# Norms of queries and keys in one chain over four steps, softmax over three, and later loads from DRAM, in a decoder trunk on one core

## The chip, the cores and the metric

The kernel runs on one core of one Trainium2 chip. The metric is the device time of one execution in microseconds, as the median of several runs; less is better. A core has a matrix engine (TensorE, PE in the profile, with PEld for its weight loads), a vector engine (VectorE, DVE), an engine for functions of one operand (ScalarE, ACT), a general one (GpSimd, POOL) and SyncE (SP), which here only issues DMAs. Each engine works through its own instructions in the order of the program, and waits on semaphores for the others. SBUF is the working memory with 128 partitions; PSUM takes the results of matmuls; DRAM holds the weights.

## The reference

One sequence of 256 tokens, 2048 features, two layers. Layer 0 is a gated mixer of tokens in chunks, layer 1 is attention with 16 heads of 128 and forget gates; a convolutional feed-forward of width 5632 follows each. The change touches the attention alone:

```python
def fox_shared_kv(h, kv_norm, w_kvf, b_f, k_norm):
    kvf = rmsnorm(h, kv_norm) @ w_kvf
    k, v, f = ...
    k = rmsnorm(k, k_norm)              # over the 128 features of each head
    c = jnp.cumsum(log_sigmoid(f + b_f), axis=1)

def forgetting_attention(xn, w_qg, q_norm, w_out, k, v, c):
    q, g = jnp.split(xn @ w_qg, 2, axis=-1)
    q = rmsnorm(q, q_norm)              # over the 128 features of each head
    s = einsum(q, k) * scale + c[t] - c[s]      # only s <= t
    p = jax.nn.softmax(s, axis=-1)
    o = einsum(p, v) * jax.nn.sigmoid(g)
    return o @ w_out
```

Queries are taken in two blocks of 128 tokens (tb = 0 and 1): the first block sees 128 keys, the second 256.

## The kernel before

**Chunks and steps.** All weights come as a stream of chunks of 128 x 1024 numbers (512 KB). `Stream.run` (L86) walks the list of items, and each item is a step. In step i it issues the load of item i + 6 on SyncE's queue (L70), splits item i + 3 into a high part `whi` on ScalarE (L82) and the rest `wlo` on VectorE (L83), issues the matmuls of item i (L166), and then lets every pending generator run to its next `yield`, in the order in which they were started (L57). A generator that is started in a chunk's matmuls runs its first piece in the same step; one that another generator starts begins a step later. An item without weights (`then`) is a place in the list where something is started, with no advance of generators. There are four buffers for loaded chunks and four each for `whi` and `wlo`. So the order of work on each engine is fixed by the order of steps, and a `yield` more in a generator moves what follows it behind the split of one further chunk.

**The attention's items.** b_q (queries, 4 blocks of 8 chunks), the chunk of forget gates, kvf_k (keys, 4 blocks of 8), a `then` that starts `heads`, kvf_v (values, 4 blocks of 8), b_g (gates), b_out. Counted from the first chunk of b_q as step 0: queries take steps 0 to 31, forget gates 32, keys 33 to 64, values 66 to 97, gates 98 to 129. A block of queries, keys or values is 256 tokens x 512 features (4 heads), with its sums in a PSUM tile `ps` of two halves (tb); there are three such tiles.

**Queries and keys** (`head_norm`, L575). When a block's last matmul is done, for each half: Square on ScalarE (L581), a sum for each of the 4 heads (L584), mean and epsilon (L585), the inverse root by one instruction on the bits (L269) and three Newton steps of three instructions (L274 to L276), the factor of the token's own norm (L587), the product into a buffer of the group `big` (L589). A step later the transpose in 32 x 32 blocks (L551) and an `exchange` (L555): four writes to DRAM (L559), one step later the read back with the blocks in transposed places (L562), one step later what is to follow, for queries the scaled copy by `q_scaled` (L604) another step later.

**Key and value operand** (`kv_operand`, L566): sixteen `prep` (L258, L259), one a step, make the normalized residual that the forget, key and value matmuls use.

**Forget gates** (`forget_sums`, L633): some 20 steps of small pieces on VectorE after step 32.

**Heads** (`heads`, L675). A head takes two steps. In the first: the difference of the forget sums into `L` (L693, L694; from a row `cB` that GpSimd's queue fetches, L683), the mask (L696), the attention output of an earlier head (L705 to L707) and its copy (L714), the scores of this head (L711, L712) into a PSUM tile of the group `mp`, of which there are two. In the second: scale and add (L718), and for the two blocks of queries the maximum (L722) and Exp with its sum (L723), then reciprocal (L725), scaling (L727), transpose and exchange, after whose read back the head is `waiting` for its output. A head's output is made when its values are there and when its number is below n - 2, n being the head whose scores are due.

**Values** (`v_evict`, L610): two copies on ScalarE (L614) after each block. **Gates** (`g_done`, L733) wait until `state["done"]` says that the two heads which they multiply are there.

Of the kernel before, what the change touches and what calls it, by code (L numbers as in the profile page):

```python
# [10 lines left out]
F32 = mybir.dt.float32  # L11
F32R = mybir.dt.float32r
I32 = mybir.dt.int32
AF = mybir.ActivationFunctionType
OP = mybir.AluOpType
AX = mybir.AxisListType

P = 128
D = 2048
T = 256  # L20
# [3 lines left out]
NH = 16  # L24
CHUNK = 1024
EPS = 1e-6
SCALE = 128 ** -0.5
# [12 lines left out]
class Stream:  # L40
# [10 lines left out]
    def then(self, at_load=None, at_split=None, at_mult=None):  # L51
        self.items.append((None, at_mult, at_load, at_split))
# [80 lines left out]
def build(ctx, tc, d, out):  # L133
    nc = tc.nc
# [3 lines left out]
    small = ctx.enter_context(tc.tile_pool(name="small", bufs=1))  # L138
# [8 lines left out]
    rcol = const.tile([P, 2], F32, name="rcol")  # L147
# [4 lines left out]
    s = Stream(nc, wpool)  # L152
    ph = Phase(tc)
# [112 lines left out]
    def rsqrt(y, v, n):  # L266

        t = small.tile([P, n], F32, name="rs_t", tag=f"rs_t{n}", bufs=2)
        nc.vector.tensor_scalar(y.bitcast(I32), v.bitcast(I32), -0.5, 1597463007.0, op0=OP.mult, op1=OP.add)  # L269
        for _ in range(3):  # L270
            newton(y, v, t)

    def newton(y, v, t):
        nc.vector.scalar_tensor_tensor(t, y, -0.5, y, op0=OP.mult, op1=OP.mult)  # L274
        nc.vector.tensor_tensor(t, t, v, op=OP.mult)  # L275
        nc.vector.scalar_tensor_tensor(y, t, 1.5, y, op0=OP.add, op1=OP.mult)  # L276
# [270 lines left out]
    def blocks_turned(src, n):  # L547


        turned = ph.temp("turned", [P, 512])[:, :n * P].rearrange("p (c h j) -> p c h j", c=4, h=n)  # L550
        nc.vector.transpose(turned.rearrange("p c h j -> p h c j"),  # L551
                            src.rearrange("p (h c i) -> p h c i", h=n, c=4))
        return turned.rearrange("p c h j -> p c (h j)")

    def exchange(key, turned, n, new, then):  # L555

        way = dram.tile([4, 32, 4, n * 32], F32, name=f"way_{key}", tag=f"way_{key}")
        for r in range(4):
            nc.sync.dma_start(way[:, :, r, :].rearrange("c i x -> i c x"), turned[32 * r:32 * r + 32])  # L559
        yield  # L560
        dst = new()
        nc.sync.dma_start(dst, way.rearrange("c i r x -> (c i) r x"))  # L562
        yield
        then(dst)

    def kv_operand():  # L566
        att("X2")
        nc.vector.tensor_tensor(att("gain"), column(C_QNORM), column(C_KNORM), op=OP.mult)
        for _ in range(3):
            yield  # L570
        for kt in range(KD):
            prep(att("X2"), kt, C_KVNORM)
            yield

    def head_norm(key, blk):  # L575

        def done(ps):
            for tb in range(2):
                x = ps[:, tb, :]
                sq = small.tile([P, 2, T], F32, name="sq", tag="sq", bufs=2).rearrange("p a b -> p (a b)")  # L580
                nc.scalar.activation(sq, x, AF.Square, scale=rcol[:, tb:tb + 1])  # L581
                v = ph.temp("hv", [P, 4])
                r = ph.temp("hr", [P, 4])
                nc.vector.tensor_reduce(v, sq.rearrange("p (a b) -> p a b", a=4), axis=AX.X, op=OP.add)  # L584
                nc.vector.tensor_scalar(v, v, 1.0 / P, EPS, op0=OP.mult, op1=OP.add)  # L585
                rsqrt(r, v, 4)
                nc.vector.tensor_scalar(r, r, rcol[:, tb:tb + 1], None, op0=OP.mult)  # L587
                n = ph.temp("big", [P, 512], bufs=6)
                nc.vector.tensor_tensor(n.rearrange("p (a b) -> p a b", a=4), x.rearrange("p (a b) -> p a b", a=4),  # L589
                                        r[:, :, None].to_broadcast([P, 4, P]), op=OP.mult)  # L590
                yield
                turned = blocks_turned(n, 4)
                if key == "k":
                    new = lambda tb=tb: att("k").rearrange("p b t h j -> p b t (h j)")[:, blk, 4 * tb:4 * tb + 4]
                    s.start(exchange(f"k{blk}{tb}", turned, 4, new, lambda dst: None))
                else:
                    s.start(exchange(f"q{blk}{tb}", turned, 4, lambda: four_rows(4),
                                     lambda dst, tb=tb: s.start(q_scaled(blk, tb, dst))))
        return done

    def four_rows(n):
        return ph.temp("rows", [P, 512], bufs=6)[:, :n * P].rearrange("p (r x) -> p r x", r=4)

    def q_scaled(blk, tb, rows):  # L604

        yield
        nc.scalar.activation(att("q")[:, 4 * blk:4 * blk + 4, tb * P:(tb + 1) * P].rearrange(
            "p h (r j) -> p r h j", r=4), rows.rearrange("p r (h j) -> p r h j", h=4), AF.Copy, scale=att("gain"))
# [66 lines left out]
    def heads():  # L675

        q, k, v, ccol = att("q"), att("k"), att("v"), att("ccol")
        parts = [(0, 0, 1), (1, 1, 3)]
        rows, waiting = {}, []

        def fetch(hd):
            rows[hd] = ph.temp("cB", [P, T])
            nc.gpsimd.dma_start(rows[hd], cd[hd:hd + 1, :].to_broadcast([P, T]))  # L683

        fetch(0)
        yield
        n = 0
        while state["done"] < NH:
            if n < NH:
                cB = rows.pop(n)  # L690
                L = ph.temp("big", [P, 512], bufs=6)[:, :3 * P]
                l = L.rearrange("p (a b) -> p a b", a=3)
                nc.scalar.activation(l[:, 0, :], cB[:, :P], AF.Identity, scale=-1.0, bias=ccol[:, 0, n:n + 1])  # L693
                nc.scalar.activation(l[:, 1:, :], cB.rearrange("p (a b) -> p a b", a=2), AF.Identity, scale=-1.0,  # L694
                                     bias=ccol[:, 1, n:n + 1])
                nc.gpsimd.affine_select(l[:, 0::2, :], l[:, 0::2, :], pattern=[[0, 2], [-1, P]],  # L696
                                        compare_op=OP.is_ge, fill=NEG, base=0, channel_multiplier=1)
                if n + 1 < NH:
                    fetch(n + 1)
            go = [hd for hd, _ in waiting if hd < min(state["v"], n - 2)][:2 if n >= NH else 1]  # L700
            o = misc_ps() if go else None
            for i, hd in enumerate(go):
                pT = waiting.pop(0)[1]
                oo, vv = o[:, i * T:(i + 1) * T], v[:, :, hd * P:(hd + 1) * P]
                nc.tensor.matmul(oo[:, :P], vv[:, 0, :], pT[:, :, 0, :], start=True, stop=True)  # L705
                nc.tensor.matmul(oo[:, P:], vv[:, 0, :], pT[:, :, 1, :], start=True, stop=False)
                nc.tensor.matmul(oo[:, P:], vv[:, 1, :], pT[:, :, 2, :], start=False, stop=True)  # L707
            if n < NH:
                S = misc_ps()[:, :3 * P]
                kk = k[:, n // 4, :, n % 4, :]  # L710
                nc.tensor.matmul(S[:, :P], q[:, n, :P], kk[:, :4], start=True, stop=True)  # L711
                nc.tensor.matmul(S[:, P:], q[:, n, P:], kk, start=True, stop=True)  # L712
            for i, hd in enumerate(go):
                nc.scalar.activation(q[:, hd, :], o[:, i * T:(i + 1) * T], AF.Copy)  # L714
                state["done"] += 1
            yield
            if n < NH:
                nc.vector.scalar_tensor_tensor(L, S, SCALE, L, op0=OP.mult, op1=OP.add)  # L718
                mx = ph.temp("mx", [P, 2])
                sm = ph.temp("sm", [P, 2])  # L720
                for tb, a, b in parts:
                    nc.vector.tensor_reduce(mx[:, tb:tb + 1], l[:, a:b, :], axis=AX.XY, op=OP.max, negate=True)  # L722
                    nc.scalar.activation(l[:, a:b, :], l[:, a:b, :], AF.Exp, bias=mx[:, tb:tb + 1],  # L723
                                         accum_out=sm[:, tb:tb + 1])
                nc.vector.reciprocal(sm, sm)  # L725
                for tb, a, b in parts:
                    nc.vector.tensor_scalar(l[:, a:b, :], l[:, a:b, :], sm[:, tb:tb + 1], None, op0=OP.mult)  # L727
                s.start(exchange(f"p{n}", blocks_turned(L, 3), 3, lambda: four_rows(3),
                                 lambda dst, n=n: waiting.append((n, dst.rearrange("p r (b j) -> p r b j", b=3)))))
            yield  # L730
            n += 1

# [17 lines left out]
    state = {"normed": False, "layer": 0, "v": 0, "done": 0, "gates": 0}  # L750
# [100 lines left out]
```

## Time and profile before

| what | us |
|---|---|
| median of 3 runs | 2222.88 (2222.6 to 2224.47) |
| profiled execution | 2217.78 |
| its span, first to last instruction | 2216.1 |
| granted clock of TensorE, mean | 0.998 |
| DVE busy | 1481.1 |
| ACT busy | 1142.3 |
| POOL busy | 24.0 |

A row of a timeline gives start and length in us, engine, line, operation, what is written and read, shapes, count, and in brackets the idle time before it with what ended it. A row of a table of windows gives the stretch and its length, then busy time and count of instructions for PE, PEld, DVE, ACT and POOL, then the granted clock of TensorE (1.00 is full), the share of the DMA engines' time and GB/s. Ends of matmuls are modelled and overlap the next one's start. A row of the waits gives the total, how often and the longest.

### The profile page before, as it was taken

Reading aid. Unit: us, or ns where it says so; the run is one execution under the profiler, and the core shown is the slowest. Engines: PE = TensorE matmul, PEld = TensorE weight load, DVE = VectorE, ACT = ScalarE, POOL = GpSimd, SP = SyncE. Lnnn points to the kernel's source line nnn. Section 1 sums busy time; section 2 is a strip of 40 time slices with the busy share of each in tenths; the row PEclk is TensorE's granted clock in tenths of the full one; section 3 lists DMA queues with packets and bytes.
Section 4 is the critical chain, followed back from the end, with each engine's and each line's share of the span. In section 5 each row is a group of like instructions: output and inputs, shape, how many; then the busy total and the mean of one; then the engine's idle time right before and its main releaser. Section 6 shows DMA issues by size and latency. Waiting matters only on the chain.

```text
span 2216.1 us, 41701 instructions
## 1 busy us (share of the span) xinstructions
PE 2193.7 (99%) x17096; PEld 2097.0 (95%) x17096; DVE 1481.1 (67%) x2140; ACT 1142.3 (52%) x1525; POOL 24.0 (1%) x41
## 2 busy tenths in 40 slices
PE   9999999999999999999999999999999999999998
PEld 8899999999999999998777888999999999999998
DVE  6667677777777655547786766667777777764553
ACT  6545455555555544435443665545555555544443
POOL 0000000000000000000000210000000000000000
PEclk9999999999999999999999999999999999999999
DMA  8555555555555555555666776555555565555653
GB/s 306 179 189 181 198 191 195 196 191 194 196 191 192 198 192 191 189 200 185 202 205 217 240 237 194 193 186 199 192 199 191 191 199 191 194 196 192 196 191 136
DMA packets 139951, 437.39 MB, mean 197 GB/s; under 512 B 24032, under 2 KB 34672, under 8 KB 139504
## 3 DMA queue, kind: packets, MB, share of 16 engines
q1 hardware_dynamic: 138816, 432.62, 58.9%
q0 software_dynamic: 768, 2.10, 0.4%
q8 instruction: 133, 2.18, 0.4%
q14 instruction: 58, 0.48, 0.1%
q10 hardware_dynamic: 176, 0.02, 0.0%
HBM read 425.22 MB, written 9.45 MB: 196 GB/s over the span
## 4 chain that ended last, share of the span: by engine, by line
PE 90%; DVE 4%; DMA 3%; issue 1%; ACT 1%; SPq 0%; ACTq 0%; DVEq 0%; POOL 0%; POOLq 0%
PE ps L166 88%; DVE wlo L83 1%; DMA raw<-kvf_k 1%; PE mp L166 1%; DMA raw<-b_q 1%; ACT whi L82 1%; DMA way_k<-att_turned 0%; DVE att_turned L551 0%; DVE att_hv L584 0%; PE mp L489 0%; DMA raw<-kvf_v 0%; DVE rs_t L275 0%; DVE rs_t L274 0%; DVE att_hr L276 0%; DMA way_q<-att_turned 0%
## 5 line engine op out<-in xcount | busy, mean ns | idle before, releaser
L83 DVE TENSOR_TENSOR wlo<-raw,whi 128x1024 fp32r<-128x1024 f32 (+1 forms) x787 | 954.1, 1218 | 455.4 <-ACT whi L82 453.6
L82 ACT ACTIVATE whi<-raw 128x1024 fp32r<-128x1024 f32 (+1 forms) x787 | 826.2, 1056 | 693.4 <-PE ps L166 590.0
L166 PE MATMUL ps<-X,whi 128*128 128x256 f32 (+1 forms) x6176 | 826.3, 285 | 0.0
L166 PEld LDWEIGHTS ps<-X,whi 128*128 128x128 f32 x6176 | 757.9, 188 | 16.2
L166 PE MATMUL ps<-X,wlo 128*128 128x256 f32 x3328 | 445.3, 276 | 0.0
L166 PEld LDWEIGHTS ps<-X,wlo 128*128 128x128 f32 x3328 | 413.0, 188 | 5.5
L166 PE MATMUL ps<-ffn_H,whi 128*128 128x256 f32 (+1 forms) x2696 | 342.9, 277 | 0.0
L166 PEld LDWEIGHTS ps<-ffn_H,whi 128*128 128x128 f32 x2696 | 322.6, 188 | 1.1
L166 PE MATMUL ps<-ffn_H,wlo 128*128 128x256 f32 x1364 | 186.7, 276 | 0.0
L166 PEld LDWEIGHTS ps<-ffn_H,wlo 128*128 128x128 f32 x1364 | 170.2, 188 | 0.4
L166 PE MATMUL ps<-whi,att_X 128*128 128x512 f32 x512 | 167.3, 403 | 0.0
L523 DVE SCALAR_TENSOR_TENSOR ffn_c<-ffn_a,col,ffn_c 128x255 f32<-128x255 f32 x352 | 162.0, 481 | 6.3
L166 PE MATMUL ps<-whi,X 128*128 128x512 f32 x512 | 160.9, 395 | 0.0
L519 ACT ACTIVATE ffn_c<-ffn_a,col 128x256 f32<-128x256 f32 x176 | 96.5, 596 | 49.7 <-DVE ffn_a L316 49.7
L166 PEld LDWEIGHTS ps<-whi,att_X 128*128 128x128 f32 x512 | 97.6, 191 | 21.1
L166 PEld LDWEIGHTS ps<-whi,X 128*128 128x128 f32 x512 | 96.6, 189 | 20.9 <-ACT whi L82 0.3
L316 DVE TENSOR_TENSOR ffn_a<-ps,rB 128x512 f32<-128x512 f32 x74 | 51.2, 692 | 96.6 <-PE ps L166 96.6
L166 PE MATMUL ps<-wlo,att_X 128*128 128x512 f32 x256 | 101.9, 398 | 6.6 <-DVE wlo L83 6.4
L166 PE MATMUL ps<-wlo,X 128*128 128x512 f32 x256 | 99.6, 392 | 5.6 <-DVE wlo L83 5.6
L258 ACT ACTIVATE X<-h,col 128x256 fp32r<-128x256 f32 x64 | 29.2, 502 | 84.6 <-DVE h L322 67.8
L166 PE MATMUL ps<-att_X,whi 128*128 128x256 f32 (+2 forms) x520 | 68.9, 281 | 0.0
L166 PEld LDWEIGHTS ps<-wlo,att_X 128*128 128x128 f32 x256 | 49.0, 191 | 19.6 <-DVE wlo L83 9.0
(156 smaller groups left out, 1152.8 us busy)
## 6 DMA issues: line engine op xcount, KB each, us to landing
raw<-up SPq DMA_DIRECT2D x352, 512.0 KB, 3.3
raw<-down SPq DMA_DIRECT2D x176, 512.0 KB, 4.3
raw<-a_in_u SPq DMA_DIRECT2D x32, 512.0 KB, 3.6
raw<-a_out SPq DMA_DIRECT2D x32, 512.0 KB, 4.1
raw<-b_q SPq DMA_DIRECT2D x32, 512.0 KB, 4.1
raw<-kvf_k SPq DMA_DIRECT2D x32, 512.0 KB, 4.7
raw<-kvf_v SPq DMA_DIRECT2D x32, 512.0 KB, 4.8
raw<-b_g SPq DMA_DIRECT2D x32, 512.0 KB, 4.2
```

Source lines behind the costliest of these rows:

```text
L82: self.nc.scalar.activation(hi[:, :n], raw, AF.Copy)
L83: self.nc.vector.tensor_tensor(lo[:, :n], raw, hi[:, :n].bitcast(F32), op=OP.subtract)
L166: nc.tensor.matmul(o, a, b, start=start, stop=stop, skip_group_check=True)
L258: nc.scalar.activation(dst[:, kt, :T], h[:, kt, :], AF.Copy, scale=g)
L316: nc.vector.tensor_tensor(a, src, rB[:, None, :].to_broadcast([P, 2, T]), op=OP.mult)
L519: nc.scalar.activation(c[:, m, :], a[:, m, :], AF.Identity, scale=w[2], bias=column(C_CONVB + l * 2 * KF + f))
L523: nc.vector.scalar_tensor_tensor(c[:, m, n:], a[:, m, :T - n], w[k], c[:, m, n:], op0=OP.mult, op1=OP.add)
```

## The change

`exchange` has one `yield` more between its writes and its read back. `kv_operand` makes sixteen preps in 24 steps. `head_norm` takes Square and sums of both halves in its first step; in the second one chain for both (8 columns); in the third and fourth a half's product, transpose and start of its exchange each. `q_scaled` waits one step more. In `heads` the softmax is a generator of its own: scale, sum and maxima a step after the scores, both Exps a step later, reciprocal, scaling and transpose a step later, and the exchange a step after that. `heads` starts its first head two steps later, and the condition that a head's output comes at least three heads after its scores is gone; it comes as soon as the read back has been issued.

```diff
@@ -558,6 +558,7 @@
         for r in range(4):
             nc.sync.dma_start(way[:, :, r, :].rearrange("c i x -> i c x"), turned[32 * r:32 * r + 32])
         yield
+        yield
         dst = new()
         nc.sync.dma_start(dst, way.rearrange("c i r x -> (c i) r x"))
         yield
@@ -570,25 +571,29 @@
             yield
         for kt in range(KD):
             prep(att("X2"), kt, C_KVNORM)
-            yield
+            for _ in range(1 + kt % 2):
+                yield
 
     def head_norm(key, blk):
 
         def done(ps):
+            v = ph.temp("hv", [P, 2, 4])
+            r = ph.temp("hr", [P, 2, 4])
+            sq = [small.tile([P, 2, T], F32, name="sq", tag="sq", bufs=2).rearrange("p a b -> p (a b)")
+                  for _ in range(2)]
             for tb in range(2):
-                x = ps[:, tb, :]
-                sq = small.tile([P, 2, T], F32, name="sq", tag="sq", bufs=2).rearrange("p a b -> p (a b)")
-                nc.scalar.activation(sq, x, AF.Square, scale=rcol[:, tb:tb + 1])
-                v = ph.temp("hv", [P, 4])
-                r = ph.temp("hr", [P, 4])
-                nc.vector.tensor_reduce(v, sq.rearrange("p (a b) -> p a b", a=4), axis=AX.X, op=OP.add)
-                nc.vector.tensor_scalar(v, v, 1.0 / P, EPS, op0=OP.mult, op1=OP.add)
-                rsqrt(r, v, 4)
-                nc.vector.tensor_scalar(r, r, rcol[:, tb:tb + 1], None, op0=OP.mult)
+                nc.scalar.activation(sq[tb], ps[:, tb, :], AF.Square, scale=rcol[:, tb:tb + 1])
+                nc.vector.tensor_reduce(v[:, tb, :], sq[tb].rearrange("p (a b) -> p a b", a=4), axis=AX.X, op=OP.add)
+            yield
+            nc.vector.tensor_scalar(v, v, 1.0 / P, EPS, op0=OP.mult, op1=OP.add)
+            rsqrt(r.rearrange("p a b -> p (a b)"), v.rearrange("p a b -> p (a b)"), 8)
+            nc.vector.tensor_tensor(r, r, rcol[:, :, None].to_broadcast([P, 2, 4]), op=OP.mult)
+            for tb in range(2):
+                yield
                 n = ph.temp("big", [P, 512], bufs=6)
-                nc.vector.tensor_tensor(n.rearrange("p (a b) -> p a b", a=4), x.rearrange("p (a b) -> p a b", a=4),
-                                        r[:, :, None].to_broadcast([P, 4, P]), op=OP.mult)
-                yield
+                nc.vector.tensor_tensor(n.rearrange("p (a b) -> p a b", a=4),
+                                        ps[:, tb, :].rearrange("p (a b) -> p a b", a=4),
+                                        r[:, tb, :, None].to_broadcast([P, 4, P]), op=OP.mult)
                 turned = blocks_turned(n, 4)
                 if key == "k":
                     new = lambda tb=tb: att("k").rearrange("p b t h j -> p b t (h j)")[:, blk, 4 * tb:4 * tb + 4]
@@ -596,6 +601,7 @@
                 else:
                     s.start(exchange(f"q{blk}{tb}", turned, 4, lambda: four_rows(4),
                                      lambda dst, tb=tb: s.start(q_scaled(blk, tb, dst))))
+            yield
         return done
 
     def four_rows(n):
@@ -603,6 +609,7 @@
 
     def q_scaled(blk, tb, rows):
 
+        yield
         yield
         nc.scalar.activation(att("q")[:, 4 * blk:4 * blk + 4, tb * P:(tb + 1) * P].rearrange(
             "p h (r j) -> p r h j", r=4), rows.rearrange("p r (h j) -> p r h j", h=4), AF.Copy, scale=att("gain"))
@@ -675,15 +682,34 @@
     def heads():
 
         q, k, v, ccol = att("q"), att("k"), att("v"), att("ccol")
-        parts = [(0, 0, 1), (1, 1, 3)]
         rows, waiting = {}, []
 
         def fetch(hd):
             rows[hd] = ph.temp("cB", [P, T])
             nc.gpsimd.dma_start(rows[hd], cd[hd:hd + 1, :].to_broadcast([P, T]))
 
+        def softmax(hd, S, L):
+            parts = [(0, L[:, :P]), (1, L[:, P:])]
+            mx = ph.temp("mx", [P, 2])
+            sm = ph.temp("sm", [P, 2])
+            nc.vector.scalar_tensor_tensor(L, S, SCALE, L, op0=OP.mult, op1=OP.add)
+            for tb, l in parts:
+                nc.vector.tensor_reduce(mx[:, tb:tb + 1], l, axis=AX.X, op=OP.max, negate=True)
+            yield
+            for tb, l in parts:
+                nc.scalar.activation(l, l, AF.Exp, bias=mx[:, tb:tb + 1], accum_out=sm[:, tb:tb + 1])
+            yield
+            nc.vector.reciprocal(sm, sm)
+            for tb, l in parts:
+                nc.vector.tensor_scalar(l, l, sm[:, tb:tb + 1], None, op0=OP.mult)
+            turned = blocks_turned(L, 3)
+            yield
+            yield from exchange(f"p{hd}", turned, 3, lambda: four_rows(3),
+                                lambda dst: waiting.append((hd, dst.rearrange("p r (b j) -> p r b j", b=3))))
+
         fetch(0)
-        yield
+        for _ in range(3):
+            yield
         n = 0
         while state["done"] < NH:
             if n < NH:
@@ -697,7 +723,7 @@
                                         compare_op=OP.is_ge, fill=NEG, base=0, channel_multiplier=1)
                 if n + 1 < NH:
                     fetch(n + 1)
-            go = [hd for hd, _ in waiting if hd < min(state["v"], n - 2)][:2 if n >= NH else 1]
+            go = [hd for hd, _ in waiting if hd < state["v"]][:2 if n >= NH else 1]
             o = misc_ps() if go else None
             for i, hd in enumerate(go):
                 pT = waiting.pop(0)[1]
@@ -710,23 +736,11 @@
                 kk = k[:, n // 4, :, n % 4, :]
                 nc.tensor.matmul(S[:, :P], q[:, n, :P], kk[:, :4], start=True, stop=True)
                 nc.tensor.matmul(S[:, P:], q[:, n, P:], kk, start=True, stop=True)
+                s.start(softmax(n, S, L))
             for i, hd in enumerate(go):
                 nc.scalar.activation(q[:, hd, :], o[:, i * T:(i + 1) * T], AF.Copy)
                 state["done"] += 1
             yield
-            if n < NH:
-                nc.vector.scalar_tensor_tensor(L, S, SCALE, L, op0=OP.mult, op1=OP.add)
-                mx = ph.temp("mx", [P, 2])
-                sm = ph.temp("sm", [P, 2])
-                for tb, a, b in parts:
-                    nc.vector.tensor_reduce(mx[:, tb:tb + 1], l[:, a:b, :], axis=AX.XY, op=OP.max, negate=True)
-                    nc.scalar.activation(l[:, a:b, :], l[:, a:b, :], AF.Exp, bias=mx[:, tb:tb + 1],
-                                         accum_out=sm[:, tb:tb + 1])
-                nc.vector.reciprocal(sm, sm)
-                for tb, a, b in parts:
-                    nc.vector.tensor_scalar(l[:, a:b, :], l[:, a:b, :], sm[:, tb:tb + 1], None, op0=OP.mult)
-                s.start(exchange(f"p{n}", blocks_turned(L, 3), 3, lambda: four_rows(3),
-                                 lambda dst, n=n: waiting.append((n, dst.rearrange("p r (b j) -> p r b j", b=3)))))
             yield
             n += 1
 
```

## The prediction

> **What bounds the kernel now.** I read the page first, then TensorE's waits, then windows of time, then the timelines of the engines around two stalls.
>
> ```profile
> span 2216.1 us, 41701 instructions
> PE 2193.7 (99%) x17096; PEld 2097.0 (95%) x17096; DVE 1481.1 (67%) x2140; ACT 1142.3 (52%) x1525; POOL 24.0 (1%) x41
> ```
> ```profile
> PE ps L166 <- DVE wlo L83: 12.0, 8, 2.9
> PE mp L711 <- DVE att_big L718: 2.2, 1, 2.2
> ```
> ```profile
> 1002.00:1030.00 28.00, 28.00 (x127) 22.98 (x127) 21.29 (x56) 15.52 (x22) 0.00 (x0) 1.00 0.59 198
> 1030.00:1246.00 216.00, 201.67 (x879) 160.85 (x878) 163.72 (x365) 97.90 (x141) 8.95 (x14) 0.98 0.66 212
> 1246.00:1330.00 84.00, 84.00 (x446) 72.04 (x445) 57.60 (x101) 52.48 (x109) 12.30 (x19) 1.00 0.76 238
> ```
>
> TensorE is the bound, so only its holes can be won. The waits (total, times, longest) put all but a trace of them in nine places, 12.0 + 2.2 = 14.2 us, and the windows show where: from 1030 to 1246 TensorE is busy 201.67 of 216 us, which is 14.3 idle; before and after it is full. That stretch is the query, forget, key and value projections, whose epilogues the change rewrites. The holes cost more than their idle time:
>
> ```profile
> 1238.52 5.50 PE ps L166 x24
> ```
> ```profile
> 1030.21 0.63 PE L166 MATMUL ps<-whi,X 128*128 128x512 f32 x2
> ...
> 1031.38 0.50 PE L166 MATMUL ps<-wlo,X 128*128 128x512 f32 x1 [0.55 <-DVE wlo L83]
> ...
> 1056.70 0.50 PE L166 MATMUL ps<-wlo,X 128*128 128x512 f32 x1 [2.85 <-DVE wlo L83]
> ...
> 1132.97 0.50 PE L166 MATMUL ps<-wlo,att_X 128*128 128x512 f32 x1 [2.02 <-DVE wlo L83]
> ...
> 1160.10 0.50 PE L166 MATMUL ps<-wlo,att_X 128*128 128x512 f32 x1 [2.46 <-DVE wlo L83]
> ```
> ```profile
> 1134.10:1137.30 3.20, 3.20 (x9) 2.55 (x8) 3.17 (x6) 0.10 (x1) 0.00 (x0) 0.50 0.96 308
> 1161.40:1164.60 3.20, 3.20 (x9) 2.51 (x8) 2.75 (x4) 0.39 (x1) 0.00 (x0) 0.50 0.92 306
> ```
>
> In the chain of waits, 24 matmuls (two chunks) take 5.50 us, so the pitch is 0.229 us and a chunk 2.75. A matmul that is followed by a hole shows 0.63 for two, 0.40 for the last: the hole is longer than its idle time by 0.17 (0.40 less the pitch), and the first matmul after it lasts 0.50 in place of 0.39. That is 0.28 for each of nine holes, 2.5 us. After two holes the granted clock (third figure from the right) is 0.50; at half clock about 3.4 us yield 1.7, so 3.4 us are lost in both. **What can be won is 14.2 + 2.5 + 3.4 = 20 us.**
>
> **Why the holes are there.** Each step splits the chunk three ahead (whi on ScalarE, wlo on VectorE), then runs one piece of each pending generator; both engines work in program order. Zero, below, is the Square of the first query block, which starts when its last matmul is done.
>
> ```profile
> 1019.65 0.69 ACT L581 ACTIVATE sq<-ps,rcol 128x512 f32<-128x512 f32 x1 [1.28 <-PE ps L166]
> ...
> 1043.06 1.06 ACT L82 ACTIVATE whi<-raw 128x1024 fp32r<-128x1024 f32 x1 [0.66 <-DMA raw<-b_q]
> ...
> 1044.43 0.67 ACT L581 ACTIVATE sq<-ps,rcol 128x512 f32<-128x512 f32 x1
> ```
> ```profile
> 1020.37 0.69 DVE L584 TENSOR_REDUCE att_hv<-sq 128x4 f32<-128x512 f32 x1 [0.75 <-ACT sq L581]
> 1021.09 0.17 DVE L585 TENSOR_SCALAR att_hv<-att_hv 128x4 f32<-128x4 f32 x1
> ...
> 1023.28 0.23 DVE L587 TENSOR_SCALAR att_hr<-att_hr,rcol 128x4 f32<-128x4 f32 x1
> 1023.61 0.69 DVE L589 TENSOR_TENSOR att_big<-ps,att_hr 128x512 f32<-128x512 f32 x1
> 1024.22 1.22 DVE L83 TENSOR_TENSOR wlo<-raw,whi 128x1024 fp32r<-128x1024 f32 x1
> 1025.35 0.48 DVE L259 SCALAR_TENSOR_TENSOR att_X<-h,col,att_X 128x256 fp32r<-128x256 f32 x1
> 1025.75 0.70 DVE L551 STREAM_TRANSPOSE att_turned<-att_big 128x512 f32<-128x512 f32 x1
> ...
> 1030.11 1.22 DVE L83 TENSOR_TENSOR wlo<-raw,whi 128x1024 fp32r<-128x1024 f32 x1
> ```
> ```profile
> 1026.53 1.81 SPq L559 DMA_DIRECT2D way_q<-att_turned  x4
> ...
> 1032.37 1.88 SPq L559 DMA_DIRECT2D way_q<-att_turned  x4
> ...
> 1036.41 0.34 SPq L562 DMA_DIRECT2D att_rows<-way_q  x1
> 1036.84 4.65 SPq L70 DMA_DIRECT2D raw<-b_q  x4
> ```
>
> First, VectorE. A chain of twelve tiny instructions (1021.09 to 1023.51, 2.4 us) runs for each half, so in two steps (5.5 us) VectorE has two splits and 2 x (0.7 + 2.4 + 0.7) of norms. The split of the chunk five after the block ends at 1031.33, which is 11.7 after zero; TensorE wanted it one pitch after the second matmul of the 1030.21 row, at 1030.67, or 11.0. The difference, 0.66, is the 0.55 hole.
>
> Second, SyncE's queue. The read back of an exchange (L562) is issued one step after its four writes (L559), and the queue stands until they have landed: the writes of 1032.37 are all issued at 1034.25, the read goes at 1036.41, and only then a bunch of four weight loads. Those come late, ScalarE waits for one until 1043.06, and the Square of the second block starts at 1044.43. Without that it would start 8 x 2.75 + 0.71 (the first hole with its losses) after 1019.65, at 1042.4: the second block starts its norms 2.0 late, and its hole is 2.85 and no longer 0.55. The later holes are these two together, and the hole at L711 is the same backlog reaching the scores: they wait for the PSUM tile that a late L718 must read.
>
> **The change, part by part.**
>
> *head_norm.* The twelve small instructions run once for both halves, on 8 columns in place of 4. No row has 8 columns; L83 shows 1024 columns at 1.22 and L551 512 at 0.70, about 1 ns a column, and L585 shows 4 at 0.17, so the chain is taken at the same 2.4 (bounds: 0 and 0.1 more). VectorE loses 8 chains, 19 us of work, none of it on the path by itself. What counts is the spread. Rebuilt from the rows above, from the same zero: Squares done at 1.3, both reductions at 2.1; split +4 at 3.5, prep 3.9, chain 6.4; split +5 at 7.6 (TensorE wants it at 11.0); prep, first product and transpose 9.2; split +6 at 10.4 (wanted 13.8); prep, second product and transpose 12.0; split +7 at 13.3 (wanted 16.5). **The margin goes from -0.7 to +3.2 us.** In the key blocks forget_sums puts its pieces there in place of the preps; I take 1 us off the margin for it. The PSUM tile is held two steps longer, 4 of the 8 steps after which one of three comes round again: no wait. *kv_operand* spreads sixteen preps over 24 steps; the operand is ready at step 25, and its first user is the forget chunk at step 32. It costs nothing.
>
> *exchange and q_scaled.*
>
> ```profile
> raw<-b_q SPq DMA_DIRECT2D x32, 512.0 KB, 4.1
> way_q<-att_turned SPq DMA_DIRECT2D x32, 64.0 KB, 3.0
> ```
>
> The read is issued a step later. Four writes take 1.81 to issue and 3.0 to land, 4.8 in all, against 2 x 2.75 = 5.5 before the read's turn, where there was 2.75. So the queue no longer stands, or stands some tenths (bound: 2 us, as now). Queued behind it are loads that need 4.1 and are wanted by ScalarE more than a step after they land. q_scaled waits one step more, which covers the later read; queries and keys come one to three steps later, and heads uses the last of them some twenty steps on.
>
> *softmax over three steps.* Scale and maxima stay in the head's second step, the two Exps go to the next, reciprocal, scaling and transpose to the one after. The attention output of a head comes after its scores by four heads where it was three (two steps), and heads begins two steps later; gates need the first two heads at step 102 and all sixteen at step 130, and the last is done at step 107. Nothing waits. A new order counts: on VectorE the former head's tail now stands ahead of L718, on which the next head's scores wait (one PSUM tile).
>
> ```profile
> 1257.00 0.40 ACT L723 ACTIVATE att_big<-att_big,att_mx 128x128 f32<-128x128 f32 x1 [2.14 <-DVE att_mx L722]
> ...
> 1257.89 1.04 ACT L82 ACTIVATE whi<-raw 128x1024 fp32r<-128x1024 f32 x1
> ```
> ```profile
> 1258.02 0.17 DVE L725 RECIPROCAL att_sm<-att_sm 128x2 f32<-128x2 f32 x1 [0.79 <-ACT att_big L723]
> ...
> 1262.03 0.55 DVE L718 SCALAR_TENSOR_TENSOR att_big<-mp,att_big 128x384 f32<-128x384 f32 x1
> ```
> ```profile
> 1257.49 0.38 PE L705 MATMUL mp<-att_rows,att_v 128*128 128x128 f32 x2
> ...
> 1264.97 0.28 PE L711 MATMUL mp<-att_k,att_q 128*128 128x128 f32 x1
> ```
> ```profile
> 1252.65 1.26 ACT L614 ACTIVATE att_v<-ps,rcol 128x512 f32<-128x512 f32 x2
> ```
>
> From 1257.49, where the chunk's matmuls end: the copy of the output at +0.9, Exps (0.9) to 2.1, whi to 3.1, wlo to 4.4, the former head's tail (1258.02 to the end of its transpose, 1.4) to 5.7, L718 to 6.3. The scores want it at 1264.97, +7.5: margin 1.2, where it was 1264.97 - 1262.58 = 2.4. Three times the eviction of a value block (1.26) falls into this and leaves nothing; I book 0.3 us for each, 1 us. The eight stalls by wlo and that of L711 go.
>
> **Sum.** 20 - 1 = 19 us. Against the profiled execution, 2217.78 us (span 2216.1 and 1.7 around it), that is 2198.8; the median of the runs shown is 2222.88, 5.1 higher, and I predict on it: 2222.9 - 19 = **2204**.
>
> [...]
>
> **Rivals.** (a) *The half-clock stretches stay*, since they come from something else than the holes. For: the longest hole had none. Against: both begin about 1 us after a hole, and the full windows have a clock of 1.00. The time: 2222.9 - (19 - 3.4) = 2207.
>
> (b) *Half stays.* SyncE still stands: writes that land in 4 to 5 us rather than 3.0 pass the 5.5, loads bunch as now, blocks begin late, and a margin of 2 to 3 us is used up in the key blocks. For: SyncE's four issues of 1.8 also have to find room. Against: the margin takes all of the 2.0 lateness seen. 2222.9 - 9.5 = 2213.
>
> (c) *It does not do what it says*: the second backlog, by loads or ScalarE's waits for rows, is the real one and the chain is merely in its shadow. Against: the first hole is explained to a tenth by the chain alone. 2222.
>
> (d) *Slower.* The tail ahead of L718 closes a loop through TensorE: scores wait for L718, L718 for the former head's Exps, these on ScalarE for the copy of an output that TensorE computes just before the scores. It decides from 1.2 us of delay; each further microsecond costs one for each of 12 heads. To end slower it must take 2 us a head, so 3.2 of delay: 2222.9 - 19 + 12 x 2.1 = 2229. Against: only a late row of forget sums or a late split could add that much.
>
> **How the numbers follow.** Forecast 0.64, (a) 0.07, (b) 0.17, (c) 0.07, (d) 0.05. The likeliest is 2204. Low end: all 20 us go and the 5.1 between median and profiled execution goes too, 2198; high end: (b) with a little more, 2214. This holds the forecast, (a) and two thirds of (b), 0.82. About 0.2% (4.4 us) is what a measurement of this kernel can tell from no change: faster is the forecast, (a) and (b), 0.88; same is (c), 0.07; slower is (d), 0.05.
>
> **What would show it.** In the profile after: TensorE's waits for wlo near 0 from 1002 to 1230, no half-clock row between 1002 and 2200, SyncE's read issues right behind a load, ScalarE's waits for b_q and kvf_k loads, as ahead of 1043.06, mostly gone, L718 ending 1 to 1.5 us ahead of L711. Waits of L711 for L718 in every head would show (d); holes before wlo with loads in bunches, (b).

## The result and the profile after

The changed kernel takes 2198.87 us (median of 4 runs, 2198.57 to 2199.32) against 2222.82 us (2222.6 to 2224.47): the ratio is 0.9891, with a 95% interval of 0.9874 to 0.9908. Its profiled execution took 2198.70 us, against 2217.78 before. The forecast was 2204, in a range of 2198 to 2214.

The page of the changed kernel, then TensorE's waits in it (total, times, longest) and a window over the rewritten stretch (columns as before: PE busy is the third figure, the granted clock the third from the right):

```profile
span 2197.0 us, 41574 instructions
PE 2187.8 (100%) x17096; PEld 2095.3 (95%) x17096; DVE 1463.5 (67%) x2044; ACT 1143.1 (52%) x1525; POOL 19.0 (1%) x41
```
```profile
PE mp L424 <- POOL ident L773: 1.5, 1, 1.5
PE ps L166 <- DVE wlo L83: 0.8, 1, 0.8
PE ps L166 <- ACT whi L82: 0.3, 1, 0.3
```
```profile
1002.00:1246.00 244.00, 244.00 (x1099) 199.05 (x1098) 181.31 (x340) 127.17 (x188) 10.16 (x20) 1.00 0.72 231
```

The three waits that are left stand in the first 13 us of the kernel. Between 1002 and 1246 TensorE is never idle, where the kernel before lost 14.3 us, and the clock is 1.00 throughout. The span fell by 19.1 us. VectorE's busy time fell by nearly as much, 17.6 us, and ScalarE's not at all, but what went is TensorE's holes: a run below (two chains) gives VectorE 15 us of that work back and loses 1.1 us.

VectorE around the end of the first query block, from the timeline after. The first Square starts at 1020.24, so that is the zero:

```profile
1020.96 1.28 DVE L586 TENSOR_REDUCE att_hv<-sq 128x4 f32<-128x512 f32 x2 [0.75 <-ACT sq L585]
1022.49 1.23 DVE L83 TENSOR_TENSOR wlo<-raw,whi 128x1024 fp32r<-128x1024 f32 x1 [0.25 <-ACT whi L82]
1023.63 0.17 DVE L588 TENSOR_SCALAR att_hv<-att_hv 128x8 f32<-128x8 f32 x1
...
1025.94 1.22 DVE L83 TENSOR_TENSOR wlo<-raw,whi 128x1024 fp32r<-128x1024 f32 x1
1027.08 0.48 DVE L259 SCALAR_TENSOR_TENSOR att_X<-h,col,att_X 128x256 fp32r<-128x256 f32 x1
1027.47 0.68 DVE L594 TENSOR_TENSOR att_big<-ps,att_hr 128x512 f32<-128x512 f32 x1
1028.19 0.71 DVE L551 STREAM_TRANSPOSE att_turned<-att_big 128x512 f32<-128x512 f32 x1
1028.83 1.18 DVE L83 TENSOR_TENSOR wlo<-raw,whi 128x1024 fp32r<-128x1024 f32 x1
...
1031.67 2.32 DVE L83 TENSOR_TENSOR wlo<-raw,whi 128x1024 fp32r<-128x1024 f32 x2
```

Read the ends of the L83 rows: the splits of the chunks five and six after the block end at 1027.16 and 1030.01, 6.9 and 9.8 after zero, and the seventh, the first of the pair in the last row, at about 12.6. TensorE wanted them at 11.0, 13.8 and 16.5, so VectorE is ahead by some 4 us where it was 0.7 behind.

SyncE's queue in the same place, and ScalarE at the next block:

```profile
1028.97 1.77 SPq L559 DMA_DIRECT2D way_q<-att_turned  x4
1030.85 0.40 SPq L70 DMA_DIRECT2D raw<-b_q  x1
1031.78 1.77 SPq L559 DMA_DIRECT2D way_q<-att_turned  x4
1033.65 0.38 SPq L70 DMA_DIRECT2D raw<-b_q  x1
1034.13 0.36 SPq L563 DMA_DIRECT2D att_rows<-way_q  x1
```
```profile
1039.47 1.06 ACT L82 ACTIVATE whi<-raw 128x1024 fp32r<-128x1024 f32 x1 [1.69 <-PE ps L166]
...
1042.22 1.27 ACT L585 ACTIVATE sq<-ps,rcol 128x512 f32<-128x512 f32 x2 [1.29 <-PE ps L166]
```

The read back (L563) follows the end of a load by 0.1 us. Over the whole stretch, 1002 to 1246, SyncE still stands before read backs for 6.8 us in all (29.1 before), which costs TensorE nothing. In these rows ScalarE waits for TensorE (`<-PE ps`) and no longer for a load; over the stretch its waits for loads fell from 45.7 to 9.1 us. The second block's Square comes at 1042.22, 8 chunks of 2.75 after the first. It was 2.0 late before.

### The profile page after: what moved, and what is told of

Same layout as the page of the kernel before. It is cut to its first block, busy times and chain, and to the rows that moved or that the text cites. A ratio compares the mean times of both kernels' runs of the same rounds, so it can differ in the third digit from the quotient of the medians.

```text
span 2197.0 us, 41574 instructions
## 1 busy us (share of the span) xinstructions
PE 2187.8 (100%) x17096; PEld 2095.3 (95%) x17096; DVE 1463.5 (67%) x2044; ACT 1143.1 (52%) x1525; POOL 19.0 (1%) x41
## 4 chain that ended last, share of the span: by engine, by line
PE 99%; DMA 0%; DVE 0%; ACT 0%; ACTq 0%; issue 0%; SPq 0%; DVEq 0%
PE ps L166 97%; PE mp L166 1%; DMA raw<-a_in_v 0%; PE mp L489 0%; PE mp L738 0%; PE mp L737 0%; PE mp L732 0%; PE mp L733 0%; PE mp L731 0%; PE mp L350 0%; DVE h L402 0%; DVE wlo L83 0%; ACT whi L82 0%; ACTq L859 0%; PE mp L290 0%
## 5 line engine op out<-in xcount | busy, mean ns | idle before, releaser
L83 DVE TENSOR_TENSOR wlo<-raw,whi 128x1024 fp32r<-128x1024 f32 (+1 forms) x787 | 954.6, 1218 | 465.1 <-ACT whi L82 458.6
L166 PEld LDWEIGHTS ps<-X,whi 128*128 128x128 f32 x6176 | 758.0, 188 | 16.3
L258 ACT ACTIVATE X<-h,col 128x256 fp32r<-128x256 f32 x64 | 29.1, 501 | 84.3 <-DVE h L322 67.8
L166 PEld LDWEIGHTS ps<-att_X,whi 128*128 128x128 f32 (+1 forms) x520 | 61.5, 185 | 2.2
```

What stands on the lines that cost most here:

```text
L83: self.nc.vector.tensor_tensor(lo[:, :n], raw, hi[:, :n].bitcast(F32), op=OP.subtract)
L166: nc.tensor.matmul(o, a, b, start=start, stop=stop, skip_group_check=True)
L258: nc.scalar.activation(dst[:, kt, :T], h[:, kt, :], AF.Copy, scale=g)
```

## The experiments

The first run asks what the runs of the kernel before differ in; the next three make one part of the change alone; then come variants of the changed kernel, and last a closer cut of the loads. All ratios are against runs of the kernel before on the same chip.

**The kernel before again**, with no edit.

> The kernel before once more, unchanged. The profiled execution of before took 2217.78 us, its timed runs 2222.6 to 2224.5. Theory: the nine holes are the same in each execution, and what differs is how many of them are followed by 3.4 us at half clock (1.7 us lost each): two in the profile shown, five in a run at 2223. So a profile at 2222 to 2224 us shows 4 to 6 such stretches and TensorE idle within 1 us of 14.2. Rival: the holes themselves are longer in the other runs; then the profile shows two stretches at half clock and idle time of some 19 us.

Measured: 2222.23 us, ratio 1.0001 (0.9992 to 1.0011). The profiled execution took 2220.65 us. Two of its windows at half clock, and TensorE's waits for VectorE and ScalarE:

```profile
1058.40:1061.60 3.20, 3.20 (x9) 2.43 (x9) 3.20 (x4) 0.67 (x1) 0.00 (x0) 0.50 0.98 330
...
1232.40:1235.60 3.20, 3.20 (x9) 2.43 (x9) 2.40 (x5) 3.20 (x7) 1.07 (x2) 0.50 0.90 287
```
```profile
PE ps L166 <- DVE wlo L83: 10.3, 6, 2.8
PE mp L711 <- DVE att_big L718: 2.5, 2, 2.2
...
PE mp L705 <- ACT att_v L614: 1.3, 1, 1.3
```

The sum is 14.1 us, 0.8 of it at the kernel's start. In the stretch from 1002 to 1246 TensorE is idle for 13.1 us, where it was 14.3, and there are four stretches at half clock, where the profile shown before has two. So the longer time does not come from longer holes: **somewhat less idle time, and more slow stretches after it.** The holes are not quite the same ones (seven against nine), and the profile fell at 2220.65 us: none was taken of this kernel at 2222 to 2224, of which the expectation speaks. The granted clock, the mean of a whole run, points the same way without a profile, but only on the average: three runs of the kernel before and of this copy at 0.998 took 2217.7 to 2219.2 us, five at 0.995 took 2222.3 to 2225.3, and the many at 0.996 between them 2217.9 to 2226.2.

**The new norms alone**, `head_norm` as in the change, the rest as before.

```diff
-            for tb in range(2):
-                nc.scalar.activation(sq, x, AF.Square, scale=rcol[:, tb:tb + 1])
...
+            for tb in range(2):
+                nc.scalar.activation(sq[tb], ps[:, tb, :], AF.Square, scale=rcol[:, tb:tb + 1])
...
+            rsqrt(r.rearrange("p a b -> p (a b)"), v.rearrange("p a b -> p (a b)"), 8)
```

> The kernel before with the new head_norm only. Theory (VectorE's chain makes the holes, SyncE's standing only adds 2.0 us of lateness, less than the new margin of 3 to 4): all holes between queries and keys go, those at the scores too or nearly; 2199 to 2205 us. Rival (late loads make the holes by themselves): the first hole goes, the others stay at 1 to 2 us each; 2210 us or more.

Measured: 2199.98 us, ratio 0.9898 (0.9881 to 0.9914). TensorE's waits:

```profile
PE mp L424 <- POOL ident L763: 1.5, 1, 1.5
PE mp L715 <- DVE att_big L722: 0.9, 1, 0.9
PE ps L166 <- DVE wlo L83: 0.8, 1, 0.8
```

Only 0.9 us at the scores is left in the stretch (the 0.8 stands at the start of the kernel, as in the changed one). One edit of three gives 22.5 of the 24 us, with SyncE's queue standing as before.

**Later reads, later q_scaled and the spread of preps alone.**

```diff
         yield
+        yield
         dst = new()
...
             prep(att("X2"), kt, C_KVNORM)
-            yield
+            for _ in range(1 + kt % 2):
+                yield
...
     def q_scaled(blk, tb, rows):
+        yield
         yield
```

> The kernel before with the later reads back, q_scaled a step later and kv_operand's spread only. Theory: every block has a hole of about 0.6 us as the first has now (split of the chunk five after, 11.7 against 11.0), so 8 x (0.6 + 0.3) = 7 us are left of the loss, with few or no stretches at half clock: 2205 to 2212 us. Rival (late loads are the real cause): 2203 us or less, holes gone but for the first.

Measured: 2211.96 us, ratio 0.9952 (0.9937 to 0.9966). Six holes of 0.8 to 2.5 us are left, 9.1 us of idle time. The time is at the upper end of the expected range, and its shape is another than expected: not eight holes of 0.6 us, but fewer and longer ones.

**The new softmax alone**, `heads` as in the change.

> The kernel before with the new heads only (softmax over three steps, first head two steps later, condition of three heads gone). Theory: the holes of query and key blocks stay, only those from 1203 on can change (1.1 + 0.2 + 2.2 of idle time, 4.3 us with their edges): 2217 to 2222 us. Rival: VectorE's and ScalarE's waits for each other in the softmax were what made the later holes of all blocks; then more than 5 us are gained.

Measured: 2221.87 us, ratio 1.0000 (0.9991 to 1.0010): no gain. The holes of the blocks stay, and one of 2.2 us at the scores too.

**The spread without the merging**: in the changed kernel, one chain for each half, both in the second step.

```diff
-            nc.vector.tensor_scalar(v, v, 1.0 / P, EPS, op0=OP.mult, op1=OP.add)
-            rsqrt(r.rearrange("p a b -> p (a b)"), v.rearrange("p a b -> p (a b)"), 8)
...
+            for tb in range(2):
+                nc.vector.tensor_scalar(v[:, tb, :], v[:, tb, :], 1.0 / P, EPS, op0=OP.mult, op1=OP.add)
+                rsqrt(r[:, tb, :], v[:, tb, :], 4)
```

> The changed kernel, but with a chain of twelve small instructions for each half, both in the second step: the spread without the merging. VectorE gets its 2.4 us a block back. Theory of the margin: in the profile after, the splits of the chunks five, six and seven after a block end 3.9 to 4.1 us before TensorE wants them, so 2.4 more make no hole: 2198 to 2200 us. Rival (what was gained is VectorE's shorter work): 8 x 2.4 = 19 us are lost again, or a good part; 2205 us or more.

Measured: 2199.95 us, ratio 0.9902 (0.9886 to 0.9919). VectorE has 2.4 us a block more to do, and it costs 1.1 us in all: one hole of 0.8 at 1147.94, in the second key block, whose norms start right after the running sum of forget_sums (1138.33).

**The merging without the spread**: chain and both products in the block's first step, both transposes in the second.

```diff
-            yield
             nc.vector.tensor_scalar(v, v, 1.0 / P, EPS, op0=OP.mult, op1=OP.add)
...
             for tb in range(2):
-                yield
                 n = ph.temp("big", [P, 512], bufs=6)
...
+            yield
+            for tb, n in enumerate(ns):
                 turned = blocks_turned(n, 4)
```

> The changed kernel with the merged chain and both products in the block's first step, both transposes in the second: the merging without the spread. Rebuilt from rows: chain done at 4.6 after the Square's start, products 5.9, split +4 at 7.1 (wanted 8.3), transposes and prep 8.9, split +5 at 10.1 (wanted 11.0). Theory: margins of 0.9 to 1.2, so no hole in query blocks, some tenths in the key blocks beside forget_sums; 2198 to 2203 us. Rival (it is the spread over four steps that counts): holes in all blocks, 2205 us or more.

Measured: 2200.38 us, ratio 0.9904 (0.9889 to 0.9919); one hole of 1.2 us in a key block. Either half of the edit is enough but for 1.1 or 1.5 us. Both variants share a third part of it, which no run takes away: both Squares stand in the block's first step. Before, ScalarE's second Square waited for VectorE's product of the first half (`ACT sq L581 <- DVE att_big L589: 24.9, 8, 4.3`). In the first block that wait cost nothing, since VectorE runs without a gap from 1020.37 to the late split; for the later blocks it is not shown.

**Three inverse roots in place of one**, with the spread.

```diff
-            rsqrt(r.rearrange("p a b -> p (a b)"), v.rearrange("p a b -> p (a b)"), 8)
+            for _ in range(3):
+                rsqrt(r.rearrange("p a b -> p (a b)"), v.rearrange("p a b -> p (a b)"), 8)
```

> The changed kernel with the merged inverse root done three times over (same result): 10 instructions twice more, 4.0 us a block more on VectorE. Theory of the margin (3.9 to 4.1 us in query blocks, about 1 less in the first key blocks, where forget_sums runs): the query blocks show no hole or tenths, the key blocks with forget_sums one of about 1 us; 2199 to 2204 us. Rival (VectorE's work counts whatever the margin): 8 x 4.0 = 32 us; rival (margin overrated): a hole of 1 to 2 us in each of eight blocks and stretches at half clock, 2210 to 2220 us.

Measured: 2214.43 us, ratio 0.9970 (0.9957 to 0.9983). **This missed.** The first block has no hole, as the margin says, but each of the seven others has one, of 0.9 to 2.5 us. The rows from ScalarE's timeline and SyncE's, after the first block:

```profile
1034.51 1.06 ACT L82 ACTIVATE whi<-raw 128x1024 fp32r<-128x1024 f32 x1 [1.90 <-DMA raw<-b_q]
...
1038.69 1.06 ACT L82 ACTIVATE whi<-raw 128x1024 fp32r<-128x1024 f32 x1 [2.72 <-DMA raw<-b_q]
1043.12 1.06 ACT L82 ACTIVATE whi<-raw 128x1024 fp32r<-128x1024 f32 x1 [3.36 <-DMA raw<-b_q]
...
1044.48 1.25 ACT L585 ACTIVATE sq<-ps,rcol 128x512 f32<-128x512 f32 x2
```
```profile
1032.94 1.77 SPq L559 DMA_DIRECT2D way_q<-att_turned  x4
1034.81 0.40 SPq L70 DMA_DIRECT2D raw<-b_q  x1
1035.74 1.75 SPq L559 DMA_DIRECT2D way_q<-att_turned  x4
1037.59 0.38 SPq L70 DMA_DIRECT2D raw<-b_q  x1
1038.07 0.39 SPq L563 DMA_DIRECT2D att_rows<-way_q  x1
1038.51 0.42 SPq L70 DMA_DIRECT2D raw<-b_q  x1
1039.64 0.32 SPq L563 DMA_DIRECT2D att_rows<-way_q  x1
1040.01 5.78 SPq L70 DMA_DIRECT2D raw<-b_q  x3
```

The first Square came at 1020.17, so the second was due at 1042.2 and is 2.3 late, behind splits that wait for loads. The read back does not hold the queue here: at 1038.07 it follows the end of a load by 0.1 us. The two loads before it are issued at 1034.81 and 1037.59, 4.0 us later than in the changed kernel (1030.85 and 1033.65), by as much as the chain grew. Two things tie them to VectorE: a load needs a buffer that the split of an earlier chunk has to free (in the kernel before, loads wait for such a split for 97.9 us between 1002 and 1246), and it stands in SyncE's order behind writes (L559) that wait for a late transpose, 1.8 us between 1032 and 1036. The trace does not part the two. The margin counted only TensorE's demand for the splits and left out this second way by which late work of VectorE comes back.

**The changed kernel with the old norms.**

> The changed kernel with the old head_norm: later reads and the new softmax without the new norms. Theory: late_alone took 2212, and the new softmax on top can only take away the holes at the scores (1.5 + 2.2 and their edges and a stretch at half clock, some 6 us): 2206 to 2212 us. Rival (norms matter only as long as loads or softmax are bad): 2202 us or less.

Measured: 2208.83 us, ratio 0.9942 (0.9927 to 0.9957). The old norms are worth 10.0 us even with everything else in place.

**The read back a step later, alone**, one line of the kernel before, and **the spread of preps alone**, the other large part of the same edit.

> The kernel before with one line: the read back of an exchange a step later. It parts late_alone, which gained 10.5 us by three edits. Theory (SyncE standing before the read back delays weight loads and with them the next block's Square by 2.0 us): most of the 10.5 comes from this line, 2212 to 2215 us, with the first hole (0.55, a thing of the chain alone) still there. Rival (three_chains showed loads late without a standing queue, since a late split frees its buffer late): the gain is less than half, 2217 us or more.

> The kernel before with kv_operand's sixteen preps over 24 steps only. Theory: one prep of 0.5 us less stands in the two steps in which the first block's splits are late, so its hole of 0.55 goes and those of the second and third block shrink by some tenths at most, the key blocks stay: 2219 to 2222 us. Rival (the spread of preps made late_alone's gain): 2215 us or less.

Measured: 2211.37 us, ratio 0.9954 (0.9939 to 0.9969), for the one line, 0.6 below the expected range; 2222.00 us, ratio 0.9998 (0.9988 to 1.0007), for the preps. The whole gain of the loads' part is this one `yield`. The first hole is there unchanged with the line (0.53 us). With the preps alone it shrinks to 0.14, much as expected, but one of 0.46 comes in the second block, and the idle time of the stretch is 16.3 us in that profile. One more thing stands in ScalarE's row with the one line, ahead of the second block's Square:

```profile
1043.33 0.71 ACT L608 ACTIVATE att_q<-att_rows,att_gain 128x512 f32<-128x512 f32 x1
1043.95 0.67 ACT L582 ACTIVATE sq<-ps,rcol 128x512 f32<-128x512 f32 x1
```

That Square was due at 1042.7 (first one at 1019.98, and 22.7 us) and comes 1.3 late, right behind a scaled copy of the first block's queries: of the 2.0 us before, 0.7 went with the queue's standing. That the other 1.3 come from the order on ScalarE is a reading of these rows; no run shows it by itself.

**The changed kernel with the old loads**, and **with the old heads.**

> The changed kernel with the old exchange, q_scaled and kv_operand. Theory: with the new norms the standing of SyncE is covered, so nothing is lost, or up to 1 us (norms_alone had 2.0 us of waits left against 0 after, 2200.0 against 2198.9 us): 2198.5 to 2200.5 us. Rival (the standing still costs a hole in blocks where forget_sums runs): 2202 us or more.

> The changed kernel with the old heads. Theory: with no backlog from the last key block the scores find their PSUM tile free even in the old order, so 2198.5 to 2200.5 us, a wait of L711 for L718 below 1 us. Rival (the old order stalls the scores by itself): 2202 us or more.

Measured: 2199.59 us, ratio 0.9898 (0.9883 to 0.9913), and 2200.90 us, ratio 0.9906 (0.9891 to 0.9921). (Of the 2.0 us of waits named in the first expectation, 1.1 stand at the kernel's start, in the changed kernel as well.) The second missed its expectation, by 0.4 us in the time and with 2.0 us of waits where less than 1 was expected. The two runs lack 0.7 and 2.0 us against the change, which the intervals of the ratios do not tell from nothing; the waits do, and in both profiles it is the scores that wait, first without the later loads, then without the new softmax:

```profile
PE mp L734 <- DVE att_big L692: 1.2, 1, 1.2
```
```profile
PE mp L718 <- DVE att_big L725: 2.0, 3, 1.3
```

No variant is faster than the changed kernel, and TensorE has no idle time left to win in this stretch.

## Why the prediction was right, and where it was off

The accounting can be tested on many profiles at once. If idle time, 0.28 us for each hole and 1.7 us for each stretch at half clock (half of the 3.41 us that each of the two in the kernel before lasts) are all that differs, what is left must be the same time in each kernel.

| profiled execution | us | idle, 1002 to 1246 | holes | half-clock stretches | what is left |
|---|---|---|---|---|---|
| before | 2217.78 | 14.3 | 9 | 2 | 2197.6 |
| before again | 2220.65 | 13.1 | 8 | 4 | 2198.5 |
| preps alone | 2223.79 | 16.3 | 9 | 4 | 2198.2 |
| softmax alone | 2220.53 | 12.3 | 8 | 5 | 2197.5 |
| three roots | 2215.41 | 13.5 | 8 | 1 | 2198.0 |
| late alone | 2211.62 | 9.4 | 6 | 2 | 2197.1 |
| old norms | 2208.01 | 7.2 | 6 | 0 | 2199.1 |
| norms alone | 2199.68 | 0.9 | 1 | 0 | 2198.5 |
| after | 2198.70 | 0.0 | 0 | 0 | 2198.7 |

(The stretches are counted as time at half clock over 3.41 us; the last column is the time less idle, 0.28 a hole and 1.7 a stretch.) It is 2197.1 to 2199.1 throughout, and 2197.4 to 2199.2 in the five profiles that are not in the table: the sum's form holds to about 2 us.

- **What can be won, 20 us of the profiled execution**: measured 2217.78 - 2198.70 = 19.1; the forecast for that execution was 2198.8.
- **The one step that failed** is "the median ... is 5.1 higher, and I predict on it: 2222.9 - 19". The term for the half clock was sized on a profile with two stretches, and runs at the median have more, as the copy's profile at 2220.65 with four of them and the runs' mean clocks show. They are part of what the change takes away, so the median fell by 24.0 and not 19, to 2198.87, the time that the sum gives for the profiled execution. How much of the 5.1 is stretches is not shown to the end: no profile of the kernel before stands at its median, the copy's four stretches stand at 2220.65, and the one at 2223.79 (preps alone) has four and 2.0 us more of idle time. The low end of the range, 2198, had this case in it, and the measured time lies only 0.9 us above it.
- **VectorE's margin**: forecast +3.4, +3.4 and +3.2 us for the three splits, measured 4.1, 4.0 and 3.9. The chain on 8 columns ran as long as on 4 (0.17 us an instruction).
- **SyncE's queue**: the read back was to be issued right behind a load; it is, and one `yield` for it is worth 11 us by itself. But norms_alone shows the queue's standing to be harmless with the new norms: there SyncE stands before read backs for 39.7 us between 1002 and 1246, more than the 29.1 of the kernel before, and TensorE is idle for 0.9. The two causes do not add up: 22.5 and 10.5 us alone, 24 together.
- **L718's margin**, 1.2 us and nothing at the eviction of a value block, with 1 us booked. The rows after (L695 is the scaling, L737 the scores; the second pair has an eviction ahead of it):

```profile
1256.20 0.52 DVE L695 SCALAR_TENSOR_TENSOR att_big<-mp,att_big 128x384 f32<-128x384 f32 x1
...
1264.17 0.52 DVE L695 SCALAR_TENSOR_TENSOR att_big<-mp,att_big 128x384 f32<-128x384 f32 x1
```
```profile
1258.16 0.39 PE L737 MATMUL mp<-att_k,att_q 128*128 128x128 f32 x2
...
1264.98 0.39 PE L737 MATMUL mp<-att_k,att_q 128*128 128x128 f32 x2
```

  It ends 1.4 and 0.3 us before the scores start, and no wait is shown: the 1 us was not paid, and rival (d) did not begin. With 0.3 us it is close, and in the changed kernel with the old loads the same scores do wait, for 1.2 us.
- **Rivals**: (a) fell: the profile after has no stretch at half clock between 1002 and 2194, and the three other runs lie within 0.7 us of it, less than the 1.7 of one stretch. What spoke for (a), a longest hole without a stretch, did not hold in the copy, where the hole of 2.79 us at the same place has one (last section). (c) fell with norms_alone. (b) did not come about. The preps cost nothing, as said.

## What to carry to other kernels

Where one engine is to be kept full, count for each burst on a helper engine by how much its next delivery is ahead of the demand, and spread or shorten the burst until that is positive; two ways to get there, here merging and spreading, are then worth little more than one. Follow a late delivery also to the buffer that it frees late, the load that waits for the buffer, and the engine that waits in order for the load, and to what stands behind it in a queue. And before a profile's sum is set against a median, ask in which terms the profiled run differs from the others: the mean clock of the runs pointed to it here.

## What the runs showed of the hardware

The same hole is followed by a stretch at half clock in one execution and not in another. In the profile shown ahead of the prediction, the hole of 2.85 us that ends at 1056.70 is followed by full clock, 1.00 from 1056.80 to 1060.00; in the copy's profile one of 2.79 at the same place is followed by half clock, 0.50 in its window from 1058.40 to 1061.60 above. The copy's matmuls after that hole:

```profile
1056.94 0.50 PE L166 MATMUL ps<-wlo,X 128*128 128x512 f32 x1 [2.79 <-DVE wlo L83]
...
1057.74 0.39 PE L166 MATMUL ps<-wlo,X 128*128 128x512 f32 x1
1057.97 0.79 PE L166 MATMUL ps<-whi,X 128*128 128x512 f32 x2
1058.56 0.63 PE L166 MATMUL ps<-wlo,X 128*128 128x512 f32 x1
```

They go from 0.39 to 0.63 us within one chunk.

Windows of the kernel before: one behind the hole of 2.85 us, then its two stretches at half clock, each with the microsecond ahead of it and the one after it (the granted clock is the third figure from the right):

```profile
1056.80:1060.00 3.20, 3.20 (x14) 2.63 (x15) 3.20 (x5) 0.00 (x0) 0.00 (x0) 1.00 0.69 210
1133.00:1134.01 1.01, 1.01 (x5) 0.84 (x6) 0.98 (x3) 0.00 (x0) 0.00 (x0) 1.00 0.11 24
1134.01:1137.42 3.41, 3.41 (x10) 2.67 (x9) 3.36 (x6) 0.21 (x1) 0.00 (x0) 0.50 0.96 301
1137.42:1138.42 1.00, 1.00 (x6) 0.84 (x5) 0.98 (x2) 0.85 (x1) 0.00 (x0) 1.00 0.86 224
1160.32:1161.32 1.00, 1.00 (x5) 0.82 (x5) 1.00 (x2) 0.00 (x0) 0.00 (x0) 1.00 0.24 53
1161.32:1164.73 3.41, 3.41 (x9) 2.65 (x9) 2.83 (x4) 0.52 (x1) 0.00 (x0) 0.50 0.98 303
1164.73:1165.73 1.00, 1.00 (x6) 0.76 (x6) 0.43 (x1) 0.54 (x1) 0.00 (x0) 1.00 0.74 232
```

Each stretch lasts 3.41 us. They begin 1.0 and 1.2 us after holes of 2.02 and 2.46 us, both shorter than the one of 2.85 that has none. What decides whether a hole is followed by one, no run shows.

Over the fourteen profiles, the longest hole between 1002 and 1246 and the granted clock of that time go together. In seven the longest is 1.8 us (old norms), 0.8 to 1.3 (five profiles) or none (the changed kernel), and the clock is 1.00. In the other seven it is 2.4 to 2.9 us, and the clock is 0.97 to 0.99. The profile with the old norms has six holes, 7.2 us of idle time and no stretch.

So a hole of 2 to 3 us was dearer here than it looks, by an estimated 1.7 us (3.41 us at a clock of 0.50) for each stretch that followed, and in one execution more than in another. The kernels here that had no stretch are those whose holes stayed at 1.8 us or less.
